# A fused decoder layer on one core: the convolution's forward transform folded, four heads' transposes moved behind v, norm sums shared with ScalarE

## The chip, the core and the metric

The kernel runs on one core of a Trainium2 chip. The metric is the device time of one execution in microseconds (us). Before the change three runs gave 284.11, 284.44 and 284.52 us, a median of 284.44. One more execution, recorded by the hardware profiler, is the one that the profile shows.

The engines are named as in the profile: PE is TensorE's matmuls (PEld its weight loads), DVE is VectorE, ACT is ScalarE, POOL is GpSimd, SP is SyncE, which issues most of the DMAs. Each engine works through its own queue in order.

## The reference

One layer over 256 tokens of width 1024, batch 1:

```python
h = rms_norm(x, norm1_g[l])
proj = h @ w_in[l]
q, k, v, u = jnp.split(proj, [ATTN_WIDTH, 2 * ATTN_WIDTH, 3 * ATTN_WIDTH], axis=-1)
...
q = apply_rope(rms_norm(q, q_norm_g[l]), cos, sin)      # 8 heads of 64
k = apply_rope(rms_norm(k, k_norm_g[l]), cos, sin)
attn = moba_attention(...)                              # 256 tokens: one block, plain causal softmax
conv = conformer_conv(u, glu_b[l], dw_w[l], dw_b[l], conv_ln_g[l], conv_ln_b[l])
x = x + jnp.concatenate([attn, conv], axis=-1) @ w_out[l]
h = rms_norm(x, norm2_g[l])
x = x + (jax.nn.silu(h @ w_gate[l]) * (h @ w_up[l])) @ w_down[l]
```

`conformer_conv` splits u (1024 wide) into a and g, forms a * sigmoid(g), convolves each of the 512 channels with its own 31 causal taps over the tokens, adds a bias, applies a layer norm over the channels and a silu. All is float32.

## The kernel before, in words

The 256 tokens stand in two blocks of 128 partitions, the second in reversed order (`_turned`, line 84). Float32 products are made of three passes: each operand is split into a rounded high part and the remainder, the low part, and high x high, high x low and low x high are summed in PSUM (`mm3`, line 323). A split costs a copy on ACT (the high part) and a subtraction on DVE (the low part); 512 columns at a time for activations, 1024 for weights (`feed`, line 280).

The projection runs as five chunks of 512 columns (line 733): k, q, the gate g, the conv input a, and v. Each chunk has eight units of six matmuls, one unit for each 128 rows of the weights, so there are 40 units. Before each unit `step()` (line 182) lets the waiting tasks go on: a task is a generator, and `yield n` puts it off by n steps. That order, with the numbers at the head of the file, is the schedule: what a task emits at a step goes to the end of each engine's queue, and `keep_order` holds it there. `feed(ahead)` then emits the splits of the weights that lie some pieces ahead.

The tasks that matter here:

- `pair_task` and `head_task` (lines 569 to 611), one for each head. The scores of two heads at a time are made on PE (`score`); DVE adds the mask and finds the maxima (line 588); ACT takes the exponentials and their sums into p (line 597); DVE makes the reciprocals (line 603); POOL scales p by them in two pieces (line 605); PE transposes p in three pieces (line 609); ACT copies the result out (line 611). p has four buffers for eight heads. Heads 0 to 3 run in steps 27 to 35, heads 4 and 5 from step 33, 6 and 7 from 34. The transposes of heads 0 and 1 stand before unit 32, 2 and 3 before unit 35, 4 and 5 before 37, 6 and 7 before 39.
- `conv_task` (line 625), from step 32. The convolution is done as a product of spectra over the tokens. It forms u = a * sigmoid(g) for block 0 in step 32 and block 1 in step 33 (lines 631, 632), splits each (high parts hh, line 633; low parts hl, lines 636 and 638), and three steps later makes two spectra of 128 rows (`spectrum`, line 643): for each, both token blocks against the table `fwd`, so six matmuls of 512 columns. `combine` (line 655) multiplies by the spectra of the taps. A third, short spectrum of block 1 alone, for the tail of the convolution, is made in `third` after v (three matmuls), and Y, the products, are split (line 678) for the way back.
- After the last unit (line 752): v is copied out of PSUM, block 0 by ACT, block 1 by DVE; `third` follows; then O, the attention output of all heads (lines 766, 767), and its split into mix.
- `ln_task` (line 680): the inverse transform (cv, three products of three matmuls). It is already folded: two sums are made, odd and even, and the two token blocks come from them as even and late by one scalar-tensor operation each (lines 695, 696). Then DVE takes each block's mean and variance (bn_stats and bn_aggr, lines 700, 701), a reciprocal root by Newton steps on two-element rows, and nb (line 705); ACT normalizes to yn (line 710); six units into the output product, PE transposes yn (cT, line 721).

The output product `po` (line 792) begins behind cv, and the feed-forward part (from line 930) fills the span from about 101 us on.

Of the kernel before, what the change touches and what calls it, by code (L numbers as in the profile page):

```python
# [16 lines left out]
P = 128  # L17
D = 1024
T = 256
# [16 lines left out]
LEAD = 4  # L36
HEAD_EXP = 1
NORM = (1, 1, 1, 1)
PT_WAIT = (4, 5, 3, 3)
S_STEP = (3, 3, 9, 9)  # L40
HF_WAIT = 3
LN_WAIT = 3
# [14 lines left out]
V_UNIT = 4 * KT + 1  # L57
V_PIECE = 22
SS_WAIT = 2
# [29 lines left out]
def _constants():  # L89


    def waves(n, t):
        ang = 2 * np.pi * ((t[:, None] * (2 * np.arange(n // 2) + 1)[None, :]) % (2 * n)) / (2 * n)
        return np.cos(ang), -np.sin(ang)

    row = np.arange(P)
    c, s = waves(T, _turned(np.arange(T)))
    ct, st = waves(2 * LAGS, LAGS - row)
    fwd = np.concatenate([c[:P], s[:P], c[P:], s[P:], np.where((row < 1) | (row > LAGS), 0.0, np.concatenate([ct, st, ct, st], 1).T).T], 1)
    fwd = _parts(fwd.astype(np.float32))  # L100
    ir, ii = waves(2 * LAGS, row + LAGS)
    tail = np.concatenate([ir, -ir, ii, ii], 1).T / LAGS * (row < LAGS)
    tail = np.concatenate([tail, (row == 0)[None], np.zeros((P - TAIL - 1, P))], 0)
    inv = _parts(np.concatenate([c[:P].T * 2 / T, np.where(row[:, None] == 0, s[P:], s[:P]).T * 2 / T, tail], 1).astype(np.float32))
    lag = TAPS - 1 - np.arange(TAPS)
    c, s = waves(T, lag)
    ct, st = waves(2 * LAGS, lag)
    fw = np.concatenate([c, s, ct, st, st, ct], 1).astype(np.float32)
    hi = _round12(fw)
    taps = np.zeros((96, 2 * P + TAIL), np.float32)  # L110
    taps[0:TAPS], taps[32:32 + TAPS], taps[64:64 + TAPS] = hi, hi, fw - hi
    out = {"fwd": fwd, "inv": inv, "taps": taps}
    at = _turned(np.arange(T))
    tri = [np.where(b[None, :] <= b[:, None], 0.0, -1e30) for b in (at[:P], at[P:])]
    out["mask"] = np.concatenate([tri[0], np.zeros((P, P)), tri[1]], 1).astype(np.float32)
    out["ident"] = np.eye(P, dtype=np.float32)
    return out
# [29 lines left out]
def _build(nc, tc, t, ctx):  # L147
# [175 lines left out]
    def mm3(out, lhs, rhs, start, stop):  # L323
        nc.tensor.matmul(out, lhs[0], rhs[0], start=start, stop=False)  # L324
        nc.tensor.matmul(out, lhs[0], rhs[1], start=False, stop=False)  # L325
        nc.tensor.matmul(out, lhs[1], rhs[0], start=False, stop=stop)  # L326

# [198 lines left out]
    def q_task(banks):  # L526
# [21 lines left out]
        nc.gpsimd.tensor_scalar(G["scq"], cqk[0], HD ** -0.5, None, op0=ALU.mult)  # L548
        for name, shape in (("fwd", [P, 2, 2 * T + TAIL]), ("inv", [P, 2, 3 * P])):
            tl = early.tile(shape, F32R, name=name)  # L550
            nc.gpsimd.dma_start(tl, t[name])
            G[name] = (tl[:, 0], tl[:, 1])
        yield S_WAIT
        G["sums"] = early.tile([P, NT, H], F32, name="sums")
        G["pT"] = [None] * H
        for j in range(H // 2):
# [12 lines left out]
    def pair_task(j):  # L569

        for i in (3, 2) if j == 2 else (j,):
            if i not in scored:
                score(i)
        banks = scored[j]
        for a in range(2):
            head = head_task(2 * j + a, banks[a], a)
            if j % 2:
                spawn(head, 1)
            else:
                next(head)  # L580
                tasks.append([now[0] + next(head), head])
        yield 0

    def head_task(h, S, odd):
# [7 lines left out]
        nc.vector.scalar_tensor_tensor(bi, mx, -1.0, scq[:, :, h], op0=ALU.mult, op1=ALU.mult)  # L592
        yield HEAD_EXP + odd
        p = work(f"p{h}", "p", 4, shape=(P, 3 * P))
        s = G["sums"][:, :, h]
        for i in range(NT):
            nc.scalar.activation(p[:, spl[i]], sm[:, spl[i]], AF.Exp, bias=bi[:, i:i + 1], scale=scq[:, i, h:h + 1],
                                 accum_out=s[:, i:i + 1])
        if h == H - 1:
            nc.scalar.activation(table, one, AF.Silu)  # L600
        yield NORM[h // 2]
        rec = work(f"rec{h}", "rec", 2, shape=(P, NT))
        nc.vector.reciprocal(rec, s)
        for i in range(NT):
            nc.gpsimd.tensor_scalar(p[:, spl[i]], p[:, spl[i]], rec[:, i:i + 1], 1.0, op0=ALU.mult, op1=ALU.mult)
        yield PT_WAIT[h // 2] - (odd if h // 2 % 2 else 0)
        b = t_bank(f"pT{h}")
        for a in range(3):
# [16 lines left out]
    def conv_task(banks):  # L625
        hh = early.tile([P, NT, W], F32R, name="hh", tag="hh")
        hl = early.tile([P, NT, W], F32R, name="hl", tag="hl")
        us = []
        for i in range(NT):
            u = work(f"ua{i}", "tmp", 6)  # L630
            nc.vector.scalar_tensor_tensor(u, banks[i], rstd1[:, i:i + 1], G["glub"][:, 0, :], op0=ALU.mult, op1=ALU.add)
            nc.vector.tensor_tensor(u, u, G["sg"][:, i, :], op=ALU.mult)
            nc.scalar.activation(hh[:, i, :], u, AF.Copy)
            us.append(u)
            if i:
                nc.vector.tensor_tensor(hl[:, 0, :], us[0], hh[:, 0, :].bitcast(F32), op=ALU.subtract)
            yield 1
        nc.vector.tensor_tensor(hl[:, 1, :], us[1], hh[:, 1, :].bitcast(F32), op=ALU.subtract)
        yield HF_WAIT
# [3 lines left out]
        def spectrum(j):  # L643
            n = spans[j][1]
            b = t_bank(f"hf{j}", "s" if j < 2 else "t")
            for i in range(NT) if j < 2 else (1,):
                o = i * T + j * P if j < 2 else 2 * T
                mm3(b[:n, :], [f[:, o:o + n] for f in fwd], (hh[:, i, :], hl[:, i, :]), i == 0 or j == 2, i == NT - 1)
            hf.append(b)

        for j in range(2):
            spectrum(j)
            yield 1
        Ws, Y = G["Ws"], G["Y"]
# [25 lines left out]
    def ln_task():  # L680
        inv = G["inv"]
        st = early.tile([P, NT, 6], F32, name="st")
        mv = early.tile([P, NT, 2], F32, name="mv")
        vv = early.tile([P, NT], F32, name="vv")
# [13 lines left out]
        cv = [even, late]  # L698
        for i in (1, 0):
            nc.vector.bn_stats(st[:, i, :], cv[i])  # L700
            nc.vector.bn_aggr(mv[:, i, :], st[:, i, :])
        nc.vector.tensor_scalar(vv, mv[:, :, 1], EPS, None, op0=ALU.add)
        lr = rsqrt(early, vv, NT, "lr")
        nb = early.tile([P, NT], F32, name="nb")
        nc.vector.scalar_tensor_tensor(nb, mv[:, :, 0], -1.0, lr, op0=ALU.mult, op1=ALU.mult)
        yield 3
# [26 lines left out]
    for chunk in range(5):  # L733
        banks = [mm_bank(f"p{chunk}{i}") for i in range(NT)]
        for kt in range(KT):
            step()
            ahead = unit // 2 + 1 if unit < L1 else (unit + 3) // 2 if unit < L2 else unit // 2 + 3
            feed(ahead if unit < V_UNIT else min(ahead, V_PIECE))
            if unit == L1 - 1:
# [13 lines left out]
    nc.scalar.activation(vs[:, 0, :], banks[0], AF.Copy, scale=rstd1[:, 0:1])  # L753
    nc.vector.tensor_scalar(vs[:, 1, :], banks[1], rstd1[:, 1:2], None, op0=ALU.mult)
    G["third"]()
# [365 lines left out]
```

## Time and profile before

| | before |
|---|---|
| runs: median (lowest to highest) | 284.44 us (284.11 to 284.52) |
| the profiled execution | 284.19 us |
| its span on the core | 282.4 us |
| PE, DVE, ACT, POOL busy | 277.7, 241.0, 208.5, 47.8 us |
| granted TensorE clock | 1.00 |
| projection up to v, tail's spectrum, O, cv | 4.6 to 77.4 us |
| output product and xT, feed-forward | from 77.4, from 101.1 us |

Rows of a timeline read: start and duration in us, engine, line, operation, output <- inputs, shapes, number of instructions merged into the row, and in brackets how long the engine had been idle and what ended that. A row that merges several instructions gives the time from the first start to the last end. Matmuls overlap, so the time that one costs is the distance between two starts, not its duration. In the table of windows a row has the window, its length, then busy time and count for PE, PEld, DVE, ACT and POOL, the granted clock, the share of the DMA engines and GB/s.

### The profile page before, as it was taken

What the parts mean: (1) busy time and instruction counts of PE and PEld (TensorE: products, weight loads), DVE (VectorE), ACT (ScalarE), POOL (GpSimd) and SP (SyncE); (2) the same over time, 40 slices, a digit from 0 to 9 for tenths busy, and PEclk for the clock granted to TensorE, in tenths of its full rate; (3) what the DMA queues carried; (4) which work ended last, traced back from release to release, by engine and by line L of the source; (5) the groups of instructions that cost most, each with busy time, mean ns of one, the idle gap of its engine ahead of it and who ended that gap; (6) DMA issues with size and microseconds to landing.
All of it is one profiled execution on the core that took longest, in us unless ns stands there. A gap on an engine that the chain in (4) does not pass through costs nothing.

```text
span 282.4 us, 4168 instructions
## 1 busy us (share of the span) xinstructions
PE 277.7 (98%) x1457; PEld 234.8 (83%) x1457; DVE 241.0 (85%) x428; ACT 208.5 (74%) x337; POOL 47.8 (17%) x75
## 2 busy tenths in 40 slices
PE   8999999999999999999999999999999999999994
PEld 6888887888788888888888888888888888888883
DVE  3979995997998869999967787698799879999995
ACT  4957579998639758567887777766678799888770
POOL 0004555633000000000111111100011221211233
PEclk9999999999999999999999999999999999999999
DMA  7999967755207771659799998995676969999544
GB/s 231 405 422 326 411 240 268 273 191 186 113 0 296 277 302 49 272 182 410 214 285 289 310 316 208 287 251 167 267 209 166 230 190 256 319 309 207 183 74 149
DMA packets 13638, 68.77 MB, mean 244 GB/s; under 512 B 1777, under 2 KB 2385, under 8 KB 7730
## 3 DMA queue, kind: packets, MB, share of 16 engines
q1 hardware_dynamic: 10162, 56.19, 53.8%
q0 software_dynamic: 3312, 12.31, 21.9%
q8 instruction: 11, 0.18, 0.2%
q14 instruction: 9, 0.07, 0.1%
q10 hardware_dynamic: 144, 0.00, 0.0%
HBM read 65.88 MB, written 2.10 MB: 241 GB/s over the span
## 4 chain that ended last, share of the span: by engine, by line
PE 98%; DVE 0%; issue 0%
PE p L746 20%; PE sum L984 19%; PE fg L313 14%; PE fu L313 14%; PE po L792 8%; PE fg L315 7%; PE fu L315 7%; PE warm L375 1%; PE S L567 1%; PE pT L609 1%; PE O L766 1%; PE xT L812 1%; PE hf L324 0%; PE hf L325 0%; PE hf L326 0%; PE cv L324 0%
## 5 line engine op out<-in xcount | busy, mean ns | idle before, releaser
L284 ACT ACTIVATE wh<-raw 128x1024 fp32r<-128x1024 f32 x81 | 84.0, 1053 | 15.8 <-PE fu L313 7.5
L232 DVE TENSOR_TENSOR wl<-raw,wh 128x1024 fp32r<-128x1024 f32 x63 | 75.9, 1219 | 5.0 <-ACT wh L284 4.9
L313 PE MATMUL fg<-g,wh 128*128 128x512 f32 x176 | 62.4, 392 | 0.0
L313 PE MATMUL fu<-g,wh 128*128 128x512 f32 x176 | 62.4, 392 | 0.0
L315 PE MATMUL fg<-g,wl 128*128 128x256 f32 x176 | 49.3, 280 | 0.0
L315 PE MATMUL fu<-g,wl 128*128 128x256 f32 x176 | 49.3, 280 | 0.0
L230 POOL DMA_DIRECT2D wl<-w x18 | 15.8, 878 | 138.3 <-ACT wl L229 66.7
L313 PEld LDWEIGHTS fg<-g,wh 128*128 128x128 f32 x176 | 32.9, 187 | 7.4 <-DVE g L820 0.2
L313 PEld LDWEIGHTS fu<-g,wh 128*128 128x128 f32 x176 | 32.9, 187 | 7.2
L315 PEld LDWEIGHTS fg<-g,wl 128*128 128x128 f32 x176 | 33.3, 189 | 0.0
L315 PEld LDWEIGHTS fu<-g,wl 128*128 128x128 f32 x176 | 33.3, 189 | 0.0
L984 PE MATMUL sum<-wh,forms 128*128 128x512 f32 x96 | 29.5, 389 | 0.0
L746 PE MATMUL p<-wh,xh 128*128 128x512 f32 x80 | 26.1, 408 | 0.0
L746 PE MATMUL p<-wh,xl 128*128 128x512 f32 x80 | 25.0, 394 | 0.0
L746 PE MATMUL p<-wl,xh 128*128 128x512 f32 x80 | 24.7, 390 | 0.0
L284 ACT ACTIVATE wh<-t 128x1024 fp32r<-128x1024 f32 x18 | 19.1, 1059 | 6.0 <-DVE t L247 3.3
L232 DVE TENSOR_TENSOR wl<-t,wh 128x1024 fp32r<-128x1024 f32 x17 | 20.8, 1222 | 1.2 <-ACT wh L284 0.8
L984 PEld LDWEIGHTS sum<-wh,forms 128*128 128x128 f32 x96 | 17.9, 188 | 3.7
L229 ACT ACTIVATE wl<-wh 128x1024 fp32r<-128x1024 f32 x19 | 20.2, 1062 | 0.6
L984 PE MATMUL sum<-wl,forms 128*128 128x512 f32 x48 | 18.7, 389 | 0.0
L746 PEld LDWEIGHTS p<-wh,xl 128*128 128x128 f32 x80 | 15.3, 191 | 3.4
L746 PEld LDWEIGHTS p<-wl,xh 128*128 128x128 f32 x80 | 15.1, 188 | 3.3
(212 smaller groups left out, 475.6 us busy)
## 6 DMA issues: line engine op xcount, KB each, us to landing
raw<-w SPq DMA_DIRECT2D x44, 1024.0 KB, 6.1
wl<-w POOLq DMA_DIRECT2D x18, 512.0 KB, 9.0
first<-first SPq DMA_DIRECT2D x8, 384.0 KB, 6.4
raw<-w SPq DMA_DIRECT2D x2, 512.0 KB, 7.0
xtok<-xtok SPq DMA_DIRECT2D x2, 512.0 KB, 9.1
x<-xtok SPq DMA_DIRECT2D x2, 512.0 KB, 6.9
kept<-x POOLq DMA_DIRECT2D x1, 1024.0 KB, 4.2
raw<-kept SPq DMA_DIRECT2D x1, 1024.0 KB, 6.4
```

The source lines that it names most:

```text
L229: nc.scalar.activation(dst[1], dst[0].bitcast(F32), AF.Copy, scale=-1.0)
L230: nc.gpsimd.dma_start(dst[1], src.bitcast(F32R), accum_op=ALU.add)
L232: nc.vector.tensor_tensor(dst[1], src, dst[0].bitcast(F32), op=ALU.subtract)
L284: nc.scalar.activation(dst[0], src, AF.Copy)
L313: nc.tensor.matmul(out.rearrange("p (a q) -> p a q", a=2), w[0], both, start=z in first and z not in seen, stop=False)
L315: nc.tensor.matmul(out[:, 0:T], w[1], both[:, 0, :], start=False, stop=z in last and left[z] == 0)
L375: nc.tensor.matmul(warm[:, 0:T], ones[:, 0:P], ones, start=True, stop=True)
L567: nc.tensor.matmul(banks[a][:, out], G["qT"][rows, j, q], G["kT"][rows, j, k], start=True, stop=True)
L609: nc.tensor.transpose(b[:, a * P:(a + 1) * P], p[:, a * P:(a + 1) * P], ident)
L746: nc.tensor.matmul(banks[i], (xh, xh, xl)[a][:, kt, sls[i]], w[a % 2], start=kt == 0 and a == 0, stop=kt == KT - 1 and a == 1)
L792: nc.tensor.matmul(po[i, n], G["mix"][l][:, k, i * P:(i + 1) * P], w[r], start=k == a == 0, stop=k == KT - 1 and a == 2)
L984: nc.tensor.matmul(banks[m], lhs, rhs, start=first, stop=last)
```

## The change

Five things change, all between units 27 and 46 of the schedule.

1. *The forward transform folds.* Both token blocks shared the same table up to signs in row 0. Now `conv_task` makes ue = u1 * minus + u0 and uo = u0 * keep + u1 (minus and keep are columns that are -1 and 1, but 0 for row 0), splits ue, uo and u1 into three high and three low parts, and each of the two spectra takes one of them alone: three matmuls, not six. The two spectra are emitted in one step (37), their banks come from the tag of the projection, and the combine follows in step 38 (it was 39). In `mm3` the second and third product change places, so that the low part of the moving operand is used last.
2. *The transposes of heads 4 to 7* are taken out of the units 37 and 39 and stand between v and the tail's spectrum; their PSUM banks are two of tag t and two of tag s.
3. *Heads 6 and 7* start in step 33 with 4 and 5 (masks, maxima and exponentials, in that order ahead of the second block's u), and their reciprocals are made in step 35, where they were in 36 and 37; the reload of ACT's table for silu now stands behind the reciprocals' lines.
4. *ScalarE* copies both blocks of v, and it makes the mean and the sum of squares of one block (late) by two passes with an accumulated sum. DVE keeps bn_stats for the other (even).
5. *The feed* of weights in the units 33 to 39 is taken back by one or two units (`V_AHEAD`).

```diff
-HEAD_EXP = 1
-NORM = (1, 1, 1, 1)
-PT_WAIT = (4, 5, 3, 3)
+EXP_WAIT = (1, 2, 1, 2, 0, 0, 0, 0)
+NORM = (1, 1, 1, 1, 1, 1, 2, 2)
+PT_WAIT = (4, 4, 5, 4)
-HF_WAIT = 3
+HF_WAIT = 2
+E_WAIT = 1
-V_PIECE = 22
+V_AHEAD = (18, 19, 19, 20, 20, 21, 22)
...
     def mm3(out, lhs, rhs, start, stop):
         nc.tensor.matmul(out, lhs[0], rhs[0], start=start, stop=False)
-        nc.tensor.matmul(out, lhs[0], rhs[1], start=False, stop=False)
-        nc.tensor.matmul(out, lhs[1], rhs[0], start=False, stop=stop)
+        nc.tensor.matmul(out, lhs[1], rhs[0], start=False, stop=False)
+        nc.tensor.matmul(out, lhs[0], rhs[1], start=False, stop=stop)
...
-        for name, shape in (("fwd", [P, 2, 2 * T + TAIL]), ("inv", [P, 2, 3 * P])):
+        for name, shape in (("fwd", [P, 2, 2 * P + TAIL]), ("inv", [P, 2, 3 * P])):
...
             head = head_task(2 * j + a, banks[a], a)
-            if j % 2:
+            if j == 1:
                 spawn(head, 1)
             else:
                 next(head)
...
-        yield HEAD_EXP + odd
+        yield EXP_WAIT[h]
...
+        yield NORM[h]
+        rec = work(f"rec{h}", "rec", 4, shape=(P, NT))
+        nc.vector.reciprocal(rec, s)
         if h == H - 1:
             nc.scalar.activation(table, one, AF.Silu)
-        yield NORM[h // 2]
-        rec = work(f"rec{h}", "rec", 2, shape=(P, NT))
-        nc.vector.reciprocal(rec, s)
         for i in range(NT):
             nc.gpsimd.tensor_scalar(p[:, spl[i]], p[:, spl[i]], rec[:, i:i + 1], 1.0, op0=ALU.mult, op1=ALU.mult)
-        yield PT_WAIT[h // 2] - (odd if h // 2 % 2 else 0)
-        b = t_bank(f"pT{h}")
+        if h < H // 2:
+            yield PT_WAIT[h]
+            turn_p(h, p)
+        else:
+            G["behind"].append((h, p))
+
+    def turn_p(h, p):
+        b = t_bank(f"pT{h}", "s" if h > 5 else "t")
         for a in range(3):
             nc.tensor.transpose(b[:, a * P:(a + 1) * P], p[:, a * P:(a + 1) * P], ident)
...
     def conv_task(banks):
-        hh = early.tile([P, NT, W], F32R, name="hh", tag="hh")
-        hl = early.tile([P, NT, W], F32R, name="hl", tag="hl")
+        hh = early.tile([P, 3, W], F32R, name="hh", tag="hh")
+        hl = early.tile([P, 3, W], F32R, name="hl", tag="hl")
...
-            nc.scalar.activation(hh[:, i, :], u, AF.Copy)
             us.append(u)
-            if i:
-                nc.vector.tensor_tensor(hl[:, 0, :], us[0], hh[:, 0, :].bitcast(F32), op=ALU.subtract)
-            yield 1
-        nc.vector.tensor_tensor(hl[:, 1, :], us[1], hh[:, 1, :].bitcast(F32), op=ALU.subtract)
+            if i == 0:
+                yield 1
+        yield E_WAIT
+        ue, uo = work("ue", "tmp", 6), work("uo", "tmp", 6)
+        nc.vector.scalar_tensor_tensor(ue, us[1], G["minus"], us[0], op0=ALU.mult, op1=ALU.add)
+        nc.scalar.activation(hh[:, 0, :], ue, AF.Copy)
+        nc.vector.scalar_tensor_tensor(uo, us[0], G["keep"], us[1], op0=ALU.mult, op1=ALU.add)
+        nc.scalar.activation(hh[:, 1, :], uo, AF.Copy)
+        nc.scalar.activation(hh[:, 2, :], us[1], AF.Copy)
+        yield 1
+        for j, u in enumerate((ue, uo, us[1])):
+            nc.vector.tensor_tensor(hl[:, j, :], u, hh[:, j, :].bitcast(F32), op=ALU.subtract)
         yield HF_WAIT
...
-            n = spans[j][1]
-            b = t_bank(f"hf{j}", "s" if j < 2 else "t")
-            for i in range(NT) if j < 2 else (1,):
-                o = i * T + j * P if j < 2 else 2 * T
-                mm3(b[:n, :], [f[:, o:o + n] for f in fwd], (hh[:, i, :], hl[:, i, :]), i == 0 or j == 2, i == NT - 1)
+            n, o = spans[j][1], j * P
+            b = mm_bank(f"hf{j}")
+            mm3(b[:n, :], [f[:, o:o + n] for f in fwd], (hh[:, j, :], hl[:, j, :]), True, True)
             hf.append(b)
         for j in range(2):
             spectrum(j)
-            yield 1
+        yield 1
...
-        for i in (1, 0):
-            nc.vector.bn_stats(st[:, i, :], cv[i])
-            nc.vector.bn_aggr(mv[:, i, :], st[:, i, :])
-        nc.vector.tensor_scalar(vv, mv[:, :, 1], EPS, None, op0=ALU.add)
+        total = early.tile([P, 3], F32, name="total")
+        rest = work("rest", "tmp", 6)
+        nc.scalar.activation(rest, late, AF.Copy, accum_out=total[:, 0:1])
+        nc.scalar.activation(total[:, 1:2], total[:, 0:1], AF.Copy, scale=-1.0 / W)
+        nc.scalar.activation(rest, late, AF.Square, bias=total[:, 1:2], accum_out=total[:, 2:3])
+        nc.vector.bn_stats(st, even)
+        nc.vector.bn_aggr(mv, st)
+        nc.vector.tensor_scalar(vv[:, 1:2], total[:, 2:3], 1.0 / W, EPS, op0=ALU.mult, op1=ALU.add)
+        nc.vector.tensor_scalar(vv[:, 0:1], mv[:, 1:2], EPS, None, op0=ALU.add)
         lr = rsqrt(early, vv, NT, "lr")
         nb = early.tile([P, NT], F32, name="nb")
-        nc.vector.scalar_tensor_tensor(nb, mv[:, :, 0], -1.0, lr, op0=ALU.mult, op1=ALU.mult)
+        nc.vector.scalar_tensor_tensor(nb[:, 0:1], mv[:, 0:1], -1.0, lr[:, 0:1], op0=ALU.mult, op1=ALU.mult)
+        nc.vector.tensor_tensor(nb[:, 1:2], total[:, 1:2], lr[:, 1:2], op=ALU.mult)
...
-            feed(ahead if unit < V_UNIT else min(ahead, V_PIECE))
+            feed(ahead if unit < V_UNIT else V_AHEAD[unit - V_UNIT])
...
     nc.scalar.activation(vs[:, 0, :], banks[0], AF.Copy, scale=rstd1[:, 0:1])
-    nc.vector.tensor_scalar(vs[:, 1, :], banks[1], rstd1[:, 1:2], None, op0=ALU.mult)
+    nc.scalar.activation(vs[:, 1, :], banks[1], AF.Copy, scale=rstd1[:, 1:2])
+    for h, p in G["behind"]:
+        turn_p(h, p)
     G["third"]()
```

The tables `fwd` and `inv` are built on the host to match; `fwd` shrinks from 632 to 376 columns in each of its two parts.

More of the change, by code (lines that the diff above doesn't have):

```diff
@@ L96, in _constants @@
     row = np.arange(P)
-    c, s = waves(T, _turned(np.arange(T)))
+    c, _ = waves(T, row)
+    _, s = waves(T, np.where(row == 0, P, row))
     ct, st = waves(2 * LAGS, LAGS - row)
-    fwd = np.concatenate([c[:P], s[:P], c[P:], s[P:], np.where((row < 1) | (row > LAGS), 0.0, np.concatenate([ct, st, ct, st], 1).T).T], 1)
+    fwd = np.concatenate([c, s, np.where((row < 1) | (row > LAGS), 0.0, np.concatenate([ct, st, ct, st], 1).T).T], 1)
     fwd = _parts(fwd.astype(np.float32))
@@ L103, in _constants @@
     tail = np.concatenate([tail, (row == 0)[None], np.zeros((P - TAIL - 1, P))], 0)
-    inv = _parts(np.concatenate([c[:P].T * 2 / T, np.where(row[:, None] == 0, s[P:], s[:P]).T * 2 / T, tail], 1).astype(np.float32))
+    inv = _parts(np.concatenate([c.T * 2 / T, s.T * 2 / T, tail], 1).astype(np.float32))
     lag = TAPS - 1 - np.arange(TAPS)
@@ L554, in q_task @@
         G["sums"] = early.tile([P, NT, H], F32, name="sums")
-        G["pT"] = [None] * H
+        G["pT"], G["behind"] = [None] * H, []
         for j in range(H // 2):
@@ L681, in ln_task @@
         inv = G["inv"]
-        st = early.tile([P, NT, 6], F32, name="st")
-        mv = early.tile([P, NT, 2], F32, name="mv")
+        st = early.tile([P, 6], F32, name="st")
+        mv = early.tile([P, 2], F32, name="mv")
         vv = early.tile([P, NT], F32, name="vv")
```

## The prediction

> **What bounds the kernel now.** I read the page first, then the table of windows, then the timelines of PE, DVE, ACT and POOL between 52 and 96 us, the only part of the span that the change touches.
>
> ```profile
> PE 277.7 (98%) x1457; PEld 234.8 (83%) x1457; DVE 241.0 (85%) x428; ACT 208.5 (74%) x337; POOL 47.8 (17%) x75
> ...
> PE 98%; DVE 0%; issue 0%
> ```
> ```profile
> 66.00:69.00 3.00, 3.00 (x15) 2.43 (x14) 1.60 (x2) 2.99 (x6) 1.24 (x3) 1.00 0.67 218
> ```
>
> The chain that ended last is TensorE alone, and in the window TensorE is busy for 3.00 of 3 us at a granted clock of 1.00, while VectorE (third figure) has 1.4 us free. So a matmul taken out is time gained, one for one, as long as nothing then arrives too late, and every new TensorE wait is time lost, one for one.
>
> **TensorE's own terms.** Its timeline, and one row of the chain:
>
> ```profile
> 59.78 0.82 PE L609 MATMUL pT<-c_ident,p 128*128 128x128 f32 x6
> ...
> 63.17 0.39 PE L324 MATMUL hf<-hh,fwd 128*128 128x512 f32 x1
> ...
> 64.58 0.82 PE L609 MATMUL pT<-c_ident,p 128*128 128x128 f32 x6
> ...
> 71.42 0.40 PE L324 MATMUL hf<-hh,fwd 128*120 128x512 f32 x1
> ...
> 72.21 0.69 PE L766 MATMUL O<-pTs,vs 128*64 128x256 f32 x3
> ...
> 75.21 0.50 PE L324 MATMUL cv<-yh,inv 128*128 128x512 f32 x1
> ...
> 85.60 1.03 PE L721 MATMUL cT<-c_ident,yn 128*128 128x128 f32 x8
> ```
> ```profile
> 64.74 0.66 PE pT L609 x6
> ```
>
> From 63.17 to 64.58 stand the six matmuls of one spectrum: 1.41 us, 0.235 each. The fold leaves three per spectrum instead of six, so over two spectra six matmuls go: **-1.41 us**. The tail's three stay. By the Trainium skill's TensorE: Matmul & The Clock Gate (Back-to-back issue gap), sustained matmuls of 512 columns are 131 ns apart, which would make this 0.79 us; by the trace they are 235 ns apart here, and the trace decides.
>
> The twelve transposes of the last four heads (0.11 each, 1.31 us) only move, from among v's matmuls to behind them: 0. They remove a wait only if one was there, and there is none to see: O starts 0.79 after the tail's spectrum, whose three matmuls take 0.70.
>
> So v ends at 71.42 - 1.41 - 1.31 = 68.70 plus any wait, the tail's spectrum starts 1.31 later, and cT would start at 85.60 - 1.41 = 84.19. The rest is whether the other engines hold these dates.
>
> **The folded input.** TensorE still reaches the first spectrum at 63.17. What stands ahead of its operands on DVE and ACT:
>
> ```profile
> 57.03 0.29 DVE L588 CUSTOM_DVE_ANT_0 sm<-S,c_mask 128x128 f32<-128x128 f32 x1
> ...
> 58.53 0.75 DVE L631 SCALAR_TENSOR_TENSOR ua<-p,c,c_rows 128x512 f32<-128x512 f32 x1
> ...
> 59.92 0.69 DVE L636 TENSOR_TENSOR hl<-ua,hh 128x512 fp32r<-128x512 f32 x1
> ...
> 61.36 0.22 DVE L603 RECIPROCAL rec<-sums 128x2 f32<-128x2 f32 x2
> ```
> ```profile
> 57.96 0.49 ACT L597 ACTIVATE p<-sm,bi,scq 128x128 f32<-128x128 f32 x1 [0.45 <-DVE bi L592]
> ...
> 60.10 0.61 ACT L633 ACTIVATE hh<-ua 128x512 fp32r<-128x512 f32 x1
> ```
> ```profile
> L618 DVE SCALAR_TENSOR_TENSOR ug<-p,c,c_rows 128x512 f32<-128x512 f32 x2 | 1.4, 736 | 0.0
> ```
>
> DVE: two heads' masks and maxima take 57.03 to 58.53, 1.50 us. All four heads now start in the same step, ahead of the second block's u, so u starts at 60.03; its two operations take 1.39 (58.53 to 59.92), the fold two operations of L618's kind, 1.4, the two reciprocals 0.1: DVE is free for the first low part at 63.0. ACT: a head's exponentials take 1.07 (57.96 to 60.10 for two). Those of heads 6 and 7 need the buffers of p2 and p3, that is the transposes at 59.78 (three of them done at about 60.3), so ACT waits for TensorE there, runs them from 60.3 to 62.5, and the high part hh0, queued behind them, is done at 63.1 (0.61 in the row). Also queued behind, and harmless so far, are the evictions of p2 and p3 and the weights of the output product. hl0 then runs 63.1 to 63.8. The new order of the three products puts hl0 last: it is wanted at 63.17 + 2 x 0.235 = 63.64 and comes at 63.9 with its wake-up. **+0.25 us**; from 0 (both queues 0.25 sooner) to 0.8 (my dates late by half an operation on each). The second spectrum's parts come 0.6 later each and wait no more. Before, DVE was past the last low part at 61.36, 1.8 us before TensorE came: the edit eats that cover whole.
>
> **Behind v.** Both evictions of v now go to ACT, and four evictions of transposes behind them:
>
> ```profile
> 67.27 0.85 ACT L611 ACTIVATE pTs<-pT 128x384 f32<-128x384 f32 x2
> ...
> 71.40 0.69 ACT L753 ACTIVATE vs<-p,c 128x512 f32<-128x512 f32 x1 [0.60 <-PE p L746]
> ...
> 72.37 1.90 ACT L213 ACTIVATE yh<-Y 128x512 fp32r<-128x512 f32 x3 [0.28 <-PE hf L326]
> ```
>
> From v's end at 68.95: vs 69.2 to 70.5, four pTs at 0.42 to 72.2, then yh, which started at 72.37 before. O starts at 71.05 and takes 3.0 (72.21 to 75.21), so heads 4 to 7 are wanted from 72.5 on: covered by the twelve transposes and the tail's spectrum. Bank reuse for the tail's spectrum is from vs or combine, both done by 70.5: 0, at most 0.3.
>
> **VectorE between the spectra and the norm.**
>
> ```profile
> 67.40 1.23 DVE L232 TENSOR_TENSOR wl<-raw,wh 128x1024 fp32r<-128x1024 f32 x1 [1.60 <-ACT wh L284]
> 68.54 0.69 DVE L657 TENSOR_TENSOR ya<-hf,Ws 128x512 f32<-128x512 f32 x1
> ...
> 69.86 0.69 DVE L659 TENSOR_TENSOR Y<-ya,yb 128x512 f32<-128x512 f32 x1
> 70.46 0.68 DVE L657 TENSOR_TENSOR ya<-hf,Ws 128x512 f32<-128x512 f32 x1
> ...
> 71.66 0.74 DVE L754 TENSOR_SCALAR vs<-p,c 128x512 f32<-128x512 f32 x1
> ...
> 76.56 0.68 DVE L691 TENSOR_TENSOR cvo<-cv,c_rows 128x512 f32<-128x512 f32 x1
> 77.55 0.75 DVE L695 SCALAR_TENSOR_TENSOR cvl<-cve,c_cols,cvo 128x512 f32<-128x512 f32 x1 [0.31 <-ACT cve L692]
> ...
> 79.80 0.69 DVE L700 BATCH_NORM_STATS2 st<-cvl 128x6 f32<-128x512 f32 x1
> 80.52 0.18 DVE L701 BATCH_NORM_AGGREGATE mv<-st 128x2 f32<-128x6 f32 x1
> ...
> 83.70 0.16 DVE L705 SCALAR_TENSOR_TENSOR nb<-mv,lr 128x2 f32<-128x2 f32 x1
> ```
> ```profile
> 84.62 0.80 ACT L710 ACTIVATE yn<-cvl,nb,lr 128x512 f32<-128x512 f32 x1
> ...
> 95.35 0.63 ACT L796 ACTIVATE sq<-x 128x512 f32<-128x512 f32 x1 [2.05 <-issue]
> ...
> 96.11 0.63 ACT L796 ACTIVATE sq<-x 128x512 f32<-128x512 f32 x1
> ```
>
> Three low parts from 63.1, 0.6 apart (as 69.86 to 70.46), and the last reciprocals bring DVE to 65.1. From a weight's low part at 67.40 to the first operation on cv at 76.56 it ran 9.16 us without idling. The change takes vs out of that run (0.66) and puts two weights' low parts in, moved there from earlier steps (1.14 each, 67.40 to 68.54): 10.8, so 75.9, and with 0.3 for two operations that GpSimd holds up (below, 0.15 each) 76.2. The block `late` follows one dependent operation on, 77.0 against 77.55. Dropping its statistics saves 0.8 (79.80 to 80.6), the doubled two-element operations give back 0.15. ACT's sums, two passes of 0.76 (95.35 to 96.11) and one tiny operation, about 1.8 us from 77.8, end at 79.6; DVE's own branch over `even`, unchanged, reaches the same point 3.2 after `late` begins (77.55 to 80.52, less a statistic, plus the wait for its own sum), at 80.2, and covers them. Two conversions of weights stand behind the sums on ACT and fit ahead of yn, which starts near 82.7. yn, done at 85.42, is then done at 85.42 - 0.55 - 0.65 = 84.2 to 84.3. TensorE wants it at 84.19 + 0.25 = 84.44. A tie with 0.2 in hand: I charge **+0.1 us**, from 0 to 0.6.
>
> **Transfers.** The feed of weights is held back two steps, so the low part that frees the next block's buffer ends near 70.7, after the combine; SP's next block waits for it, and the two loads of x behind that.
>
> ```profile
> 66.18 0.90 SPq L777 DMA_DIRECT2D x<-xtok  x2
> ```
> ```profile
> 94.51 1.28 DVE L801 TENSOR_TENSOR x<-po,x 128x512 f32<-128x512 f32 x2
> ```
>
> x goes out 4.5 us later than at 66.18 and is wanted at 94.5: 0; uncovered, it would cost those 4.5. The shorter spectrum table only shrinks a load issued in q's stage, long before.
>
> **Sum.** -1.41 + 0.25 + 0.1 = -1.06. The profiled execution took 284.19 us (282.4 of span, 1.8 around it), so 283.1; from the median of the runs, 284.44, it is 283.4. I say 283.2.
>
> **Rivals.** *GpSimd is late with p7.* Its scalings and VectorE side by side:
>
> ```profile
> 54.98 2.33 POOL L605 TENSOR_SCALAR p<-p,rec 128x128 f32<-128x128 f32 x2
> ...
> 61.72 1.66 POOL L605 TENSOR_SCALAR p<-p,rec 128x128 f32<-128x128 f32 x4 [4.41 <-ACT wh L284]
> ```
> ```profile
> 55.06 0.84 DVE L632 TENSOR_TENSOR ua<-ua,sgt 128x512 f32<-128x512 f32 x1
> 55.82 1.21 DVE L232 TENSOR_TENSOR wl<-raw,wh 128x1024 fp32r<-128x1024 f32 x1
> ```
>
> Undisturbed, two heads take 1.66. But the two operations from 54.98 ended only at 57.31, 0.28 after a back-to-back pair of VectorE operations with both inputs in SBUF, and the first of that pair took 0.84 instead of 0.69: each blocks the other. Under the change the reciprocals of heads 4 and 5 come at 63.0, and from 63.1 VectorE runs hl0, hl1, hl2 and a weight's low part on end, to 66.3. If GpSimd slips in nowhere, its first scaling ends at 66.55 and three more by 67.8; Y0 (67.6 to 68.4) holds the fifth to 68.65, and the eighth would start at 69.45, just as the next low part is due (69.4 to 69.5). Lost, that race means waiting for two low parts and Y1, to 72.75, where TensorE wants p7 at 68.95 + 9 x 0.11 = 69.9: +2.8, with the -1.16 left of the fold +1.65, 285.8. It decides at 0.1 us. For it: the trace's 2.33. Against: one scaling done in any earlier gap (at the reciprocals, or while hl0 waits for hh0) wins it by 0.5. The Trainium skill states such a rule: in SBUF — State Buffer (Who interferes with whom) a VectorE instruction with two SBUF inputs and a GpSimd instruction that reads SBUF shut each other out for the whole instruction, issue order deciding; by that rule this rival stands, and the trace's 2.33 agrees.
>
> *The slack is overdrawn elsewhere.* hh0 comes later than 63.1, or VectorE, now without a gap from 57 to 77 us, reaches the norm late, and TensorE waits 0.5 to 1.3 us more, at hf or at cT: 283.6 to 284.5. For: both dates are ties. Against: the operations are all in the rows.
>
> *The change does less than it says*, since all of it was hidden: 284.4. Against: TensorE is never idle there.
>
> **How the numbers follow.** Forecast 0.62 (282.7 to 283.6 by itself); overdrawn slack 0.18; GpSimd 0.16; no effect 0.04. About 0.2%, 0.57 us, is what the measurement can tell from no change. Faster: 0.62 and 0.04 of the second; same: 0.12 of the second and the last, 0.16; slower: GpSimd and 0.02 of the second. The range 282.7 to 284.9 leaves out mostly GpSimd's case.
>
> **What would show it.** Right: nine hf matmuls; about 0.25 us between the second and third of the first spectrum; twelve transposes on end behind v; cT near 84.4. Wrong: a scaling of over 1.5 us ending past 70, with TensorE still before p7's transposes; ACT exponentials of head 6 past 62; yn after cT's turn.

## The result, and the profile after

| | before | after |
|---|---|---|
| measured together: median (lowest to highest), runs | 284.25 us (283.66 to 284.52), 6 | 282.44 us (282.38 to 283.04), 6 |
| measured together once more | 283.95 us (283.55 to 284.80), 23 | 282.68 us (282.37 to 282.94), 6 |
| the profiled execution, its span | 284.19, 282.4 us | 283.04, 281.3 us |

The ratio is 0.9945 (95% interval 0.9930 to 0.9959), the second time 0.9954 (0.9941 to 0.9967). By these ratios the change is faster by some 1.3 to 1.6 us, 0.5% (the medians of the first set lie 1.81 apart, those of the second 1.27). The prediction said 283.2 us and 282.7 to 284.9: the direction was right, and the median lies 0.26 us under the range's low end.

The page of after, busy time and chain:

```profile
PE 276.5 (98%) x1451; PEld 232.6 (83%) x1451; DVE 241.6 (86%) x430; ACT 210.6 (75%) x344; POOL 49.6 (18%) x75
...
PE 97%; DMA 1%; ACT 0%; DVE 0%; issue 0%
```

Six matmuls fewer, PE busy for 1.2 us less, and the chain is still TensorE's (the DMA percent is the very first load). So the result can be read from TensorE's starts alone. TensorE's timeline of after:

```profile
63.41 0.50 PE L326 MATMUL hf<-hh,fwd 128*128 128x512 f32 x1
63.74 0.40 PE L327 MATMUL hf<-hh,fwd 128*128 128x512 f32 x1
64.13 0.51 PE L328 MATMUL hf<-hl,fwd 128*128 128x512 f32 x1
64.48 0.39 PE L326 MATMUL hf<-hh,fwd 128*128 128x512 f32 x1
...
65.20 0.62 PE L769 MATMUL p<-wh,xh 128*128 128x512 f32 x2
...
69.30 1.47 PE L617 MATMUL pT<-c_ident,p 128*128 128x128 f32 x12
70.52 0.48 PE L326 MATMUL hf<-hh,fwd 128*120 128x512 f32 x1
...
71.40 0.66 PE L791 MATMUL O<-pTs,vs 128*64 128x256 f32 x4
...
74.20 0.50 PE L326 MATMUL cv<-yh,inv 128*128 128x512 f32 x1
...
84.70 1.03 PE L744 MATMUL cT<-c_ident,yn 128*128 128x128 f32 x8
...
95.15 1.03 PE L837 MATMUL xT<-c_ident,x 128*128 128x128 f32 x8
...
101.53 1.03 PE L837 MATMUL xT<-c_ident,x 128*128 128x128 f32 x8
...
108.76 0.39 PE L315 MATMUL fg<-g,wh 128*128 128x512 f32 x1
```

The same view of before, for the rows that the prediction did not need:

```profile
96.15 1.03 PE L812 MATMUL xT<-c_ident,x 128*128 128x128 f32 x8
...
102.53 1.04 PE L812 MATMUL xT<-c_ident,x 128*128 128x128 f32 x8
...
109.84 0.40 PE L313 MATMUL fg<-g,wh 128*128 128x512 f32 x1
```

One more view fixes the origin: the chain in order of time (start, duration, what). First before, then after; then the two kernels again in the second measurement, the kernel before first.

```profile
4.58 29.55 PE p L746 x126
34.12 0.87 PE qT L516 x8
```
```profile
4.62 29.73 PE p L769 x126
34.36 0.87 PE qT L518 x8
```
```profile
34.06 0.87 PE qT L516 x8
```
```profile
33.91 0.87 PE qT L518 x8
```

The 126 matmuls of the k and q chunks and the first units of g, which the change does not touch and which run while the first loads come in, took 29.55 us in one execution and 29.73 in the other; qT came at 34.12, 34.36, 34.06 and 33.91. From qT on the executions of one kernel repeat to about 0.1 us (rest of the span: 282.4 - 34.12 = 248.28 and, in the second execution of before, 282.3 - 34.06 = 248.24; after: 246.94, then 280.9 - 33.91 = 246.99). So in these four executions the scatter inside the span sits ahead of qT, and the change is worth 1.34 and 1.25 us by its traces. Runs scatter outside of the span too: the second execution of before took 284.66 us with a span of 282.3, the first 284.19 with 282.4. Where the change gains, by the starts above:

| stretch, from start to start | before | after | difference | predicted |
|---|---|---|---|---|
| qT to the first spectrum | 29.05 | 29.05 | 0 | 0 |
| first spectrum to O | 9.04 | 7.99 | -1.05 | -1.41 + 0.25 = -1.16 |
| O to cv | 3.00 | 2.80 | -0.20 | 0 |
| cv to cT | 10.39 | 10.50 | +0.11 | +0.10 |
| cT to the first xT | 10.55 | 10.45 | -0.10 | 0 |
| first to second xT | 6.38 | 6.38 | 0 | 0 |
| second xT to the same matmul late in the first gate and up products (109.84, 108.76) | 7.31 | 7.23 | -0.08 | 0 |
| sum | | | -1.32 | -1.06 |

What TensorE's weight loads waited for between 58 and 106 us (engine, line, what it waited for: us in total, times, longest), in before and then in after. Left out are two waits of 0.2 that both kernels have, at cv's first matmul and at the feed-forward part's:

```profile
PEld O L766 <- ACT vs L753: 0.4, 1, 0.4
PEld po L792 <- DVE mixl L214: 0.2, 1, 0.2
...
```
```profile
PEld hf L328 <- DVE hl L655: 0.4, 1, 0.4
PEld O L791 <- ACT pTs L619: 0.4, 1, 0.4
PEld cv L328 <- DVE yl L216: 0.3, 1, 0.3
PEld hf L326 <- ACT hh L649: 0.3, 1, 0.3
...
```

A weight load runs ahead of its matmul, so its wait is longer than what TensorE loses; the table above has the loss. Three waits are new here (hh and hl at the spectra, yl at cv), one is gone (mixl, behind cT), and the gain at O shows in no wait at all.

### The profile page after: what moved, and what is told of

The parts are those of the page before. It is cut to its first block, busy times and chain, and to the rows that moved or that the text cites. A ratio compares the mean times of both kernels' runs of the same rounds, so it can differ in the third digit from the quotient of the medians.

```text
span 281.3 us, 4160 instructions
## 1 busy us (share of the span) xinstructions
PE 276.5 (98%) x1451; PEld 232.6 (83%) x1451; DVE 241.6 (86%) x430; ACT 210.6 (75%) x344; POOL 49.6 (18%) x75
## 4 chain that ended last, share of the span: by engine, by line
PE 97%; DMA 1%; ACT 0%; DVE 0%; issue 0%
PE p L769 20%; PE sum L1009 19%; PE fg L315 15%; PE fu L315 14%; PE po L817 8%; PE fg L317 7%; PE fu L317 7%; DMA first<-first 1%; PE S L569 1%; PE pT L617 1%; PE O L791 1%; PE xT L837 1%; PE hf L328 0%; PE cv L326 0%; PE cT L744 0%; PE O L792 0%
## 5 line engine op out<-in xcount | busy, mean ns | idle before, releaser
L769 PEld LDWEIGHTS p<-wh,xh 128*128 128x128 f32 x80 | 14.7, 191 | 3.9 <-issue 0.7
```

Of the source, the lines that this page charges most:

```text
L769: nc.tensor.matmul(banks[i], (xh, xh, xl)[a][:, kt, sls[i]], w[a % 2], start=kt == 0 and a == 0, stop=kt == KT - 1 and a == 1)
```

## The experiments

The theory: the fold takes its 1.41 us off TensorE, and the other parts (feed, copies of v on ScalarE, transposes behind v, sums on ScalarE) only keep other engines' dates, each worth the wait that comes back without it; O's 0.20 us comes from the copies of v. Rivals: the fold pays by itself; the surplus over the prediction is scatter; the new waits are avoidable, so that a better order beats the change. Ratios are to the kernel before, measured in the same session on the same chip.

**The two kernels again.** No edit.

> The kernel before, unchanged, against itself: how far two sets of runs of one kernel lie apart. Theory A (the change is worth what the two traces show from the first transposes of q on, 1.34 us; the rest of the 1.81 us between the medians is scatter between runs): a ratio within 0.1% of 1 but single runs up to 0.8 us apart, and a trace in which the time from the first transpose of q to the end is again 248.4 us while the time before it differs. Theory B (the change takes 0.4 to 0.5 us more than that somewhere, for good): a ratio of 1.000 with single runs within 0.3 us.

> The changed kernel, unchanged. Theory A: 1.3 us under the kernel before, ratio 0.9953, and in the trace 247.07 us from the first transpose of q to the end. Theory B: 1.8 us under it, ratio 0.9937, and a stretch of the trace outside of 60 to 110 us that is shorter than before.

Before against itself 0.9999 (0.9988 to 1.0009), medians 283.93 and 283.95 us over 12 and 23 runs. After 0.9954 (0.9941 to 0.9967), 282.68 us. That is Theory A of both texts: the surplus of the first set's medians is scatter. Their 248.4 and 247.07 us count from the first transposition of q itself, 0.16 ahead of the chain's row; by that count the new traces show 282.3 - 33.90 = 248.40 in before and 280.9 - 33.75 = 247.15 in after. In the two later measurements the kernel before took 284.05 (33 runs) and 284.09 (11 runs). The 284.44 of the first three runs was high by about 0.4.

**The fold alone**, in the kernel before (the order of the three products with it):

```diff
-HF_WAIT = 3
+HF_WAIT = 2
+E_WAIT = 1
...
+        nc.vector.scalar_tensor_tensor(ue, us[1], G["minus"], us[0], op0=ALU.mult, op1=ALU.add)
...
+        nc.vector.scalar_tensor_tensor(uo, us[0], G["keep"], us[1], op0=ALU.mult, op1=ALU.add)
...
+            mm3(b[:n, :], [f[:, o:o + n] for f in fwd], (hh[:, j, :], hl[:, j, :]), True, True)
```

> The fold alone (part 1, with the new order in mm3) in the kernel before; heads, transposes, feed, copies of v and norm sums as before. My working says that VectorE then has ue, uo, the masks and maxima of heads 6 and 7 and a weight's low part ahead of the first low part of the spectra, which comes near 64.8 us, where TensorE wants it at 63.6: a wait of 1.2 us there, so -1.41 + 1.2 = -0.2 us (within 0.3 of the kernel before). Rival (the six matmuls are the whole of it, the other parts are dressing): -1.4 us.

1.0014 (1.0003 to 1.0024), 284.32 us: the gain is gone, and a little more, where 0.2 us of gain was expected. Some 0.1 of the loss lies outside of the span (1.95 us a run, 1.84 in before, by the medians). TensorE's timeline:

```profile
65.07 0.50 PE L328 MATMUL hf<-hl,fwd 128*128 128x512 f32 x1 [1.35 <-DVE hl L649]
```

and VectorE's rows there:

```profile
63.21 1.21 DVE L234 TENSOR_TENSOR wl<-raw,wh 128x1024 fp32r<-128x1024 f32 x1
64.34 0.68 DVE L649 TENSOR_TENSOR hl<-ue,hh 128x512 fp32r<-128x512 f32 x1
```

The six matmuls saved are given back by one wait: the matmul at 65.07 comes 1.74 us after the one ahead of it, not 0.235, and the next one 0.34 later. A weight's low part and the masks of two heads still stand ahead of hl0 on VectorE. The rival that the fold pays by itself is out. The new order of the three products was not tried without the fold.

**The new feed taken out of the change**, so that the weights' low parts come as early as before:

```diff
-            feed(ahead if unit < V_UNIT else V_AHEAD[unit - V_UNIT])
+            feed(ahead if unit < V_UNIT else min(ahead, 22))
```

> The changed kernel with the feed of weights at its old units (34, 36, 38). A low part of 1.14 us then stands on VectorE ahead of the spectra's first low part: TensorE waits 1.1 us more at the first spectrum, so about 1.1 us over the changed kernel. Rival (VectorE's work is only put in another order, it is the sum up to cv that counts): less than 0.3 us over the changed kernel, because the wait at the spectra is given back at cv.

0.9982 (0.9974 to 0.9991), 283.53 us: 0.8 of the gain lost, where 1.1 was expected.

```profile
64.45 0.51 PE L328 MATMUL hf<-hl,fwd 128*128 128x512 f32 x1 [0.97 <-DVE hl L655]
```

The two spectra take 2.74 us from start to start where after's took 1.79 (63.41 to 65.20); at cv 0.12 to 0.18 come back, because one low part fewer stands ahead of yl.

**The transposes of heads 4 to 7 left among v's matmuls**, the rest of the change as it is:

```diff
-PT_WAIT = (4, 4, 5, 4)
+PT_WAIT = (4, 4, 5, 4, 3, 3, 4, 4)
...
-        if h < H // 2:
-            yield PT_WAIT[h]
-            turn_p(h, p)
-        else:
-            G["behind"].append((h, p))
+        yield PT_WAIT[h]
+        turn_p(h, p)
```

> The changed kernel, but the transposes of heads 4 to 7 back among v's matmuls (units 37 and 39). By the lock between VectorE and GpSimd p5 is ready at 67.3 us in the changed kernel, where TensorE would want it at 65.2: a wait of 2.0 us before unit 37, so about 1.9 us over the changed kernel, slower than the kernel before by 0.1 to 0.6. Rival (moving them only changes the place): as the changed kernel, within 0.2 us.

1.0048 (1.0032 to 1.0064), 285.35 us: slower than before, and 2.7 over the changed kernel, where 1.9 was expected.

```profile
PEld pT L614 <- POOL p L607: 2.1, 3, 1.1
PEld O L788 <- ACT vs L773: 0.5, 1, 0.5
```

The wait of 2.0 for GpSimd's scalings was expected (2.1 by this list); what was not is that O, with no transposes ahead of it to cover the copies of v, waits for both of them and takes 3.33 us. So the move is worth 2.7 us within the change; what it is worth in the schedule of before, together with the copies, the next run shows.

**The transposes and the copies of v alone**, in the kernel before (the two spectra there take banks of the projection's tag, as in the change); and **the change with VectorE copying the second block of v again**:

```diff
-    nc.vector.tensor_scalar(vs[:, 1, :], banks[1], rstd1[:, 1:2], None, op0=ALU.mult)
+    nc.scalar.activation(vs[:, 1, :], banks[1], AF.Copy, scale=rstd1[:, 1:2])
+    for h, p in G["behind"]:
+        turn_p(h, p)
...
```
```diff
-    nc.scalar.activation(vs[:, 1, :], banks[1], AF.Copy, scale=rstd1[:, 1:2])
+    nc.vector.tensor_scalar(vs[:, 1, :], banks[1], rstd1[:, 1:2], None, op0=ALU.mult)
```

> The kernel before with the transposes of heads 4 to 7 behind v and both copies of v on ScalarE (spectra in the projection's banks); no fold, feed and norm sums as before. My prediction put this part at 0. New theory: in the kernel before, the second matmul of O waits for VectorE's copy of v (72.40 us), so the first head's pass runs alone and the two column halves of the array stay out of step; O takes 3.00 us instead of 2.80. With twelve transposes as cover the pairs start together: O 2.80 us and the kernel about 0.2 us faster. Rival (the 0.2 us comes from the fold's earlier spectra): O 3.00 us, no change.

> The changed kernel with the second block of v copied by VectorE, as before. VectorE's queue holds two low parts of weights ahead of that copy, which would end near 73.0 us where ScalarE had it at 70.7; O waits for it: about 1.3 us over the changed kernel, so level with the kernel before. Rival (the copy is short and hidden on either engine): as the changed kernel, within 0.2 us.

The first: 0.9992 (0.9982 to 1.0001), no difference clear of the noise in the time of a run. But O takes 2.81 us in its trace, where after's took 2.80, with both spectra as in before, and the gain stands in the spans: 281.9 us in the mean of its 11 runs, 282.2 in that of before's 33, 0.28 apart (95% interval 0.10 to 0.46). Outside of the span it spends 2.04 us, not 1.84 (medians), which hides this; the reason is open. The fold does not do it: in fold_only, which has neither of the two edits, O takes 2.97. The second: 1.0011 (1.0001 to 1.0020), 284.36 us, 1.7 over the changed kernel where 1.3 was expected; O takes 4.42. TensorE's timeline of the second:

```profile
71.24 0.65 PE L791 MATMUL O<-pTs,vs 128*64 128x256 f32 x2
72.91 0.32 PE L792 MATMUL O<-pTs,vs 128*64 128x128 f32 x1 [1.02 <-DVE vs L777]
72.91 0.43 PE L791 MATMUL O<-pTs,vs 128*64 128x256 f32 x1
```

Each matmul of O runs as two passes (16 records of each line for eight heads), and two heads of 64 columns share the array. Here the first head's two passes run, its second matmul waits for block 1 of v, and the next head's first matmul, which needs only block 0, stands behind it. The same happens in before on a small scale. O's first moments (a timeline cut off some 0.05 to 0.25 us after O's start), in before and in after:

```profile
72.21 0.43 PE L766 MATMUL O<-pTs,vs 128*64 128x256 f32 x1
```
```profile
71.40 0.44 PE L791 MATMUL O<-pTs,vs 128*64 128x256 f32 x2
```

In its first 0.2 us before has one pass under way; after has two within 0.05. Block 1 of v is ready in before at 71.66 + 0.74 = 72.40; the second head starts at 72.48, 0.27 us after the first, and the two stay out of step to the end. Neither edit gives this alone within the change: with the copies on ScalarE but no transposes as cover (the run above) O takes 3.33, with the cover but VectorE's copy 4.42. The Trainium skill's TensorE: Matmul & The Clock Gate (Why this matters for your kernels) says that matmuls whose outputs lie in different column groups run at the same time; after's trace agrees, its pairs starting 0.01 us apart.

**VectorE makes the statistics of both blocks again:**

```diff
-        nc.scalar.activation(rest, late, AF.Copy, accum_out=total[:, 0:1])
...
-        nc.scalar.activation(rest, late, AF.Square, bias=total[:, 1:2], accum_out=total[:, 2:3])
-        nc.vector.bn_stats(st, even)
...
+        for i in (1, 0):
+            nc.vector.bn_stats(st[:, i, :], cv[i])
...
```

> The changed kernel with both blocks' norm sums on VectorE again. The chain to yn gets 0.65 us longer; yn was done 0.3 us before TensorE took it, so TensorE waits about 0.4 us at cT (0.2 to 0.6 over the changed kernel). Rival (the norm sums are hidden under the output product): no difference, no gap before cT.

0.9980 (0.9971 to 0.9989), 283.52 us, 0.8 over the changed kernel.

```profile
PEld cT L738 <- ACT yn L727: 0.5, 1, 0.5
...
PEld po L811 <- DVE mixl L216: 0.4, 1, 0.4
```

About the expected 0.4 us (0.38 by the starts) at cT, and some 0.3 more behind it: ScalarE's two conversions of weights, queued behind yn, come later too, and behind them the copy of cT's result. A date of yn counts twice, and the second time was in no theory. Another 0.1 of the 0.8 lies outside of the span (1.91 us a run, 1.78 in after, by the medians).

**The reciprocals of heads 6 and 7 three steps later**, so that GpSimd's last four scalings start while VectorE makes the low parts of two weights:

```diff
-NORM = (1, 1, 1, 1, 1, 1, 2, 2)
+NORM = (1, 1, 1, 1, 1, 1, 5, 5)
```

> The changed kernel with the reciprocals of heads 6 and 7 three steps later, behind the combine and straight ahead of two low parts of weights and Y1 on VectorE. If VectorE operations with two SBUF inputs lock GpSimd's scalings out (the rival of the prediction), p6 and p7 are ready only after 73.3 and 74.6 us, TensorE stands ahead of their transposes, and the kernel takes 4.0 to 4.5 us more than the changed one; a scaling of over 3 us in the trace. Without a lock the four scalings take 1.7 us from 70.2 on: 1.4 to 1.7 us over the changed kernel.

1.0128 (1.0113 to 1.0143), 287.67 us, 5.0 over the changed kernel, where 4.0 to 4.5 was expected. GpSimd, VectorE, a wait, and from the page the granted clock in 40 slices of the span (a digit is in tenths of full speed, 9 is 90% or more; the 7 is the slice from 71.5 to 78.6 us):

```profile
69.45 4.01 POOL L607 TENSOR_SCALAR p<-p,rec 128x128 f32<-128x128 f32 x4 [2.27 <-DVE rec L603]
```
```profile
69.26 2.34 DVE L234 TENSOR_TENSOR wl<-raw,wh 128x1024 fp32r<-128x1024 f32 x2
```
```profile
PEld pT L617 <- POOL p L607: 3.6, 4, 2.4
```
```profile
PEclk9999999999799999999999999999999999999999
```

Four scalings take 4.01 us, where four undisturbed ones took 1.66 (in the prediction): the first of them alone lasts 2.32 (69.45 to 71.77), 0.17 past the end of the two low parts. The transposes take 5.02 us where after's took 1.22, and O and the tail's spectrum lose 1.2 more. That is the prediction's GpSimd rival made to happen, at 5.0 us instead of its 2.8. TensorE's idle time ahead of the transposes is 2.17 + 0.56 = 2.73 us, about the rival's 2.8. The rest is mostly the clock, which neither the rival nor the expectation had: behind this idle time the granted clock falls, to a mean of 0.70 from 72.6 to 73.8 us and to 0.50 from 73.8 to 76.3 us, and it is 1.00 again from 78 us. The tail's spectrum and the start of O stand there; 3.4 us at half clock (an estimate from these means) are 1.7 us lost. In fold_only and vs_dve, with 1.35 and 1.02 us of idle time, it stays at 1.00.

**Heads 6 and 7 started and normed as in before**, with the transposes behind v:

```diff
-EXP_WAIT = (1, 2, 1, 2, 0, 0, 0, 0)
-NORM = (1, 1, 1, 1, 1, 1, 2, 2)
+EXP_WAIT = (1, 2, 1, 2, 0, 0, 1, 2)
+NORM = (1, 1, 1, 1, 1, 1, 1, 1)
...
-            if j == 1:
+            if j % 2:
```

> The changed kernel with heads 6 and 7 one step later again (masks and maxima behind u of the second block, exponentials and reciprocals in the steps that follow, one head a step). VectorE's work ahead of the first low part is the same, so TensorE's wait at the spectra too, and p7 is ready near 68 us, well before its transposes: within 0.2 us of the changed kernel. Rival (the sooner reciprocals are what lets the transposes start on time): 0.3 us or more over it, with a wait ahead of p6's or p7's transposes.

0.9952 (0.9941 to 0.9964), 282.68 us: as the change. The wait for hl0 is longer (0.7 in the list of waits, 0.4 in after), and the wait for yl at cv is gone. Behind v the later scalings are still in time, so the third part of the change is worth nothing that shows.

**The spectra a step later**, with one weight's low part moved to fit; and the same **with the second product Y made ahead of the two weights' low parts and split first**:

```diff
-HF_WAIT = 2
+HF_WAIT = 3
-V_AHEAD = (18, 19, 19, 20, 20, 21, 22)
+V_AHEAD = (18, 19, 19, 20, 20, 20, 22)
```
```diff
-        second = combine(1)
+        combine(1)()
...
-            second()
...
-        for j in range(3):
+        for j in (1, 0, 2):
```

> The changed kernel with the spectra one unit later (and the feed of two pieces behind the combine, so that VectorE's order stays). TensorE's wait of 0.36 us for the spectra's first low part goes. If VectorE, without a gap from 57 us to cv, sets the pace, the wait comes back at cv and at cT: within 0.15 us of the changed kernel, and the wait at cv grows by 0.3. If the wait at the spectra is a cost by itself: 0.36 us under the changed kernel.

> As the kernel with the later spectra, and besides Y1 straight behind its products, ahead of the two low parts of weights, and the way back split in the order in which cv takes it (1, 0, 2). That brings cv's first low part 0.5 us forward on VectorE without adding work, so the wait does not come back at cv: 0.2 to 0.4 us under the changed kernel, with up to 0.3 us of wait at cT instead. Rival (the wait at cT takes all of it): as the changed kernel.

0.9966 (0.9954 to 0.9979), 283.25 us, and 0.9961 (0.9948 to 0.9973), 283.14 us: no gain on the change, and for the second 0.2 to 0.4 us was expected. In the first, hf waits for nothing (1.39 us for both spectra, which brings O forward by 0.42 against qT) and cv for more (cv to cT 10.94, in after 10.50); in the second, cv's wait is nearly gone, and cT and mixl wait (cT to the first xT 11.05, in after 10.45):

```profile
74.93 0.50 PE L328 MATMUL cv<-yl,inv 128*128 128x512 f32 x1 [0.28 <-DVE yl L216]
```
```profile
PEld cT L743 <- ACT yn L732: 0.5, 1, 0.5
PEld po L816 <- DVE mixl L216: 0.4, 1, 0.4
```

Three orders, nearly one sum: from the first transposition of q on, the traces take 247.26 and 247.34 us, where after took 247.10 and 247.15; the medians of the two, 0.6 and 0.5 over the change, are of five runs that lie up to 0.7 apart. VectorE, which runs from 57 us to the first operation on cv without a gap, sets the pace, and TensorE's slack only moves along. The rival that the new waits are avoidable is out for these two orders. No version here beats the change.

## Why the prediction was wrong

Its steps in their order.

**Six matmuls, -1.41: right.** The spectra have nine matmuls, and fold_only shows the same three per spectrum.

**The wait for hl0, +0.25: right in place and cause, 0.13 small.** The rows ask 63.41 + 2 x 0.235 = 63.88 for the third matmul, and it came at 64.13: 0.25 late, but the match is partly luck. 0.10 of it was lost one matmul earlier: the second came 0.33 after the first (63.41 to 63.74), because the first weight load had waited for hh0 and could not run ahead. In fold_only, where it did not wait, the second came 0.24 after the first. The wait for hl0 by itself is 64.13 - 63.74 - 0.235 = 0.155. ScalarE's and VectorE's timelines of after:

```profile
62.74 0.62 ACT L649 ACTIVATE hh<-ue 128x512 fp32r<-128x512 f32 x1
```
```profile
63.39 0.69 DVE L655 TENSOR_TENSOR hl<-ue,hh 128x512 fp32r<-128x512 f32 x1
...
64.60 0.78 DVE L655 TENSOR_TENSOR hl<-ua,hh 128x512 fp32r<-128x512 f32 x1
...
69.97 2.34 DVE L234 TENSOR_TENSOR wl<-raw,wh 128x1024 fp32r<-128x1024 f32 x2
...
73.44 1.88 DVE L216 TENSOR_TENSOR yl<-Y,yh 128x512 fp32r<-128x512 f32 x3
...
76.45 0.68 DVE L706 TENSOR_TENSOR cvo<-cv,c_rows 128x512 f32<-128x512 f32 x1
```

hh0 ends at 63.36 and hl0 starts at 63.39; forecast 63.1 for both, and this execution ran 0.24 later from qT on. So the dates were right. What the sum lacked is the restart: behind the wait for hl0 the next matmul comes 0.35 later (64.13 to 64.48), not 0.235, and the second one's delay behind hh0 is another. Both spectra take 1.79, 0.38 over six matmuls.

**The transposes moved, 0: right for their own time. "They remove a wait only if one was there, and there is none to see": this failed.** Twelve on end take 1.22 (69.30 to 70.52). But move_vs shows 0.2 us that went at O with these two edits; the prediction's "O starts at 71.05 and takes 3.0" carried it over. It was not in the trace as idle time: TensorE was busy with one head of two. It stood in the rows all the same: block 1 of v was ready at 72.40, after O's start at 72.21, and O's rows in before show three passes and then one where after has four and four.

**VectorE's long run, first operation on cv at 76.2: right** (76.45 - 0.24 = 76.21). But only its end was followed. Two weights' low parts stand in it ahead of yl, and cv's third product waits for yl: cv to cT +0.11. The same edit that pays at hf costs there; old_feed gives that wait back.

**The tie at cT, +0.1: the dates were right, the charge was not due.** ScalarE's timeline of after:

```profile
83.61 0.80 ACT L733 ACTIVATE yn<-cvl,nb,lr 128x512 f32<-128x512 f32 x1
```

yn ends at 84.41 and cT starts at 84.70, on time; forecast, 0.24 added, 84.44 to 84.54 and 84.68. no_sums, the same kernel without ScalarE's sums, shows what was at stake: 0.7. The two sides nearly cancel by chance: +0.10 was charged at cT, +0.11 came at cv.

**Behind cT, 0: missed by -0.10.** In before yn ended 0.18 ahead of cT's start (85.42 to 85.60), in after 0.29. ScalarE's conversions and mixl move with it, and the wait for mixl in before's list is gone. no_sums moves the same wait the other way.

**Feed-forward, 0: missed by -0.08 to -0.1, cause open.** The same 40 matmuls stand a few ns closer. From the second xT to the next matmul behind these 40 (prb) it takes 7.93 to 7.94 us in after (twice), fold_only, no_move, old_feed, vs_dve and no_sums, and 8.03 to 8.04 in before (twice), move_vs, rec_late, old_heads, hf_late_feed and y_first. What separates the two groups was not tried.

**GpSimd's rival: its rule right, and here it was missed by 0.4 us.** GpSimd's timeline of after, whole and cut off at 64 us:

```profile
63.46 6.09 POOL L607 TENSOR_SCALAR p<-p,rec 128x128 f32<-128x128 f32 x8 [6.01 <-ACT hh L649]
```
```profile
63.46 1.38 POOL L607 TENSOR_SCALAR p<-p,rec 128x128 f32<-128x128 f32 x1 [6.01 <-ACT hh L649]
```

Eight scalings, held to 789 ns each in the mean where the four undisturbed ones of before took 445, end at 69.55; the next weights' low parts begin at 69.97. The first ends at 64.84, behind hl0 and hl1 and inside hl2, and this third hl took 0.78, not 0.68: GpSimd got in there once, as the prediction said one gap would do. rec_late shows the other side; its price of 2.8 was right for the wait and left out the clock.

**The base: this failed too.** "I say 283.2" lies between the sum from one profiled execution (283.1) and from the median of three runs (283.4). Taken from 283.95 to 284.09, the medians of 23, 33 and 11 runs, the same sum gives 282.9 to 283.0; with the -1.32 of the trace, 282.6 to 282.8, where the change was measured at 282.44 and 282.68. So of the half microsecond between 283.2 and 282.68, 0.26 is the undersized gain (-0.20 at O, -0.10 behind cT, -0.08 in the feed-forward part, against +0.11 at the spectra and +0.01 from cv to cT) and about 0.25 the base. The range's low end, 282.7, allowed for a smaller wait at hf and none at cT, and held no gain that is not a wait in the trace.

## What to carry to other kernels

A fold that takes work off the busiest engine is worth what the feeding engine's queue allows: here the same edit cost 0.4 us alone and is the core of a gain of 1.3 with the feed moved out of its way, and each later order that removed one wait found it again one stage on. Look for lost time in a busy engine too: where two instructions should share it, check that the operand of each is ready before the first starts. And before a change of 1 us is forecast to 0.2, find out which part of a run scatters, inside of the span and outside of it, and take the base from more than three runs.

## What the runs showed of the hardware

- Two heads' matmuls of 64 columns run side by side when both can start; one that starts 0.27 us late costs 0.20 us over 32 passes, since they do not fall back into step (3.00 against 2.80 us).
- Scalings on GpSimd against back-to-back operations of two inputs on VectorE: 4.01 us for four instead of 1.66, the first held for 2.32. By the Trainium skill's SBUF — State Buffer (Who interferes with whom) the one that issues first keeps the other out for a whole instruction; here it was kept out for two operations in a row, by the low parts of two weights in rec_late and by hl0 and hl1 in after, where it then ended during the third, hl2.
- Behind a matmul that waited, or whose weight load did, the next one came 0.33 to 0.35 us later, not 0.235 (63.41 to 63.74 and 64.13 to 64.48 in after).
- TensorE's granted clock fell to 0.50 for some 3.4 us behind 2.17 and 0.56 us of idle time (rec_late); behind 1.35 us (fold_only) it stayed at 1.00.
- The scatter of a run lies in part in its first 34 us (qT from 33.91 to 34.36 in four executions) and in part outside of the span (1.74 to 2.36 us in the same four); from qT on two executions of one kernel agree to 0.1 us in 248.
